# Two-layer hybrid block with expert lookup: the context tokens' routing moves beside the merge of the latent tokens, and GpSimd's adds and multiplies move to VectorE

## The chip, the cores and the metric

The kernel runs on one core of one Trainium2 chip. The metric is the time of one execution in microseconds (us). Before the change it is 4922.6 us (median of three runs, 4914.19 to 4927.8). The engines are TensorE (PE; its weight loads are PEld), VectorE (DVE), ScalarE (ACT), GpSimd (POOL) and SyncE (SP), which issues most of the transfers. The whole computation is in 32-bit floats.

## The reference, cut to what matters

There are 256 context tokens and 512 latent tokens, of width 1024, and two layers. In a layer each kind of token is normalized, projected, sent through three mixers (a state-space scan, differential attention, neighbourhood attention), and the three results are merged. After that comes an expert layer: every token scores 16,384 experts, takes the best 16 for each of 8 heads, and adds the weighted rows of those experts. In layer 1 only the latent tokens go on after the mixers.

```python
def merge_branches(y_ssm, y_diff, y_na, g_ssm, g_diff, g_na, w_br_ssm, w_br_diff, w_br_na, w_out):
    m = (sigmoid(g_ssm) * (y_ssm @ w_br_ssm) + sigmoid(g_diff) * (y_diff @ w_br_diff)
         + sigmoid(g_na) * (y_na @ w_br_na))
    return m @ w_out

def peer_ffn(h, wq, subkeys, u_tab, v_tab):              # h: normalized tokens
    q = (h @ wq).reshape(..., 8, 2, 128)
    s = einsum('bchxd,hxnd->bchxn', q, subkeys)           # scores of 128 + 128 half keys per head
    sv, si = top_k(s, 16)
    cand = sv[..., 0, :, None] + sv[..., 1, None, :]
    best, pos = top_k(cand, 16)
    eidx = take_along_axis(si0 * 128 + si1, pos)
    g = softmax(best)
    act = gelu(einsum('bchkd,bcd->bchk', u_tab[eidx], h))
    return einsum('bchk,bchkd->bcd', g * act, v_tab[eidx])

# in each layer, for latents (and for the context in layer 0):
x  = x + g1 * merge_branches(...)
h2 = rmsnorm(x, norm2_g) * (1 + sc2) + sh2
x  = x + g2 * peer_ffn(h2, ...)
```

## The kernel before, in words

**Arithmetic.** A 32-bit matmul operand is cut in two parts: ScalarE writes the rounded part `hi` (line 61) and VectorE the rest `lo = raw - hi` (line 62). `mm3` (lines 70 to 72) then runs three matmuls, hi by hi, lo by hi and hi by lo. Weights come in chunks of 128x1024 through a ring of `raw` tiles on SP's queue; `stream(3, 4)` gives three `raw` tiles and four pairs of parts. Each chunk therefore costs one transfer of 512 KB, one `hi` on ScalarE and one `lo` on VectorE before TensorE can use it.

**Stages of layer 0.** By the trace: a start (to 183 us), the mixers (to about 800), the merge (to 1093), a transition in which the tokens are normalized again (to 1138), the early stage (to about 2221), and the experts (to 2985). Layer 1 goes through the same stages with the latents alone.

**The merge** (`merge`, lines 924 to 972) works on one kind of tokens at a time, the 256 context tokens first (group 0), then the 512 latents (group 1). The mixer outputs are split into `yh` and `yl`. For each of eight blocks of 128 output columns, the three branches are multiplied by their weights (`w_br`), VectorE multiplies the result by the gate (line 946, tile `g`), and GpSimd adds the three (lines 947 and 948). The sum is split again into `mh` and `ml`, multiplied by `w_out`, scaled on VectorE (line 968, tile `d`) and added to the residual `x` on GpSimd (line 969). Beside the merge of layer 0, `modulation` multiplies 24 chunks of `ada_w` for layer 1; they use the same ring. The ring passes 80 chunks in this stage.

**The early stage** runs two things beside each other. `early` multiplies the latents by the 128 chunks of the expert table `peer_u` (tile `s`). `routing` first treats the context: normalization (`prepared`), queries with the 16 chunks of `peer_wq` (for 256 columns) and the scores of the half keys (`chosen`), the search for the best 16 by VectorE's maximum instructions (lines 1026 to 1033), the candidates and the lookup of their indices (`route`, lines 1064 to 1175), which leaves `picks`. Then it does the queries of the latents, and beside these `gathered` fetches for every pick of the context a row of the expert table per token: GpSimd issues an indirect transfer into one of five `grow` buffers (line 1200), and VectorE multiplies it with the token and sums (line 1214 for the first table, line 1222 for the second). What is left of the gathering goes on beside the experts.

**What sets the order.** `weave` draws pieces from several generators in proportion to the costs that they yield and to a budget for each. The order in which pieces are emitted and the framework's scheduler give every engine one list of instructions, which is fixed before the run. Instructions whose tiles share memory wait for one another; that includes transfers.

**Complex products** (`cmul`, lines 236 to 247, used in the start and the mixers) take six instructions; VectorE does four, and GpSimd a multiply (line 243) and, in most calls, an add (line 247).

Of the kernel before, what the change touches and what calls it, by code (L numbers as in the profile page):

```python
# [9 lines left out]
F32 = mybir.dt.float32  # L10
F32R = mybir.dt.float32r
# [10 lines left out]
LCTX, LLAT = 256, 512  # L22
# [28 lines left out]
class Net:  # L51
# [183 lines left out]

    def cmul(self, o, x, y, t, neg=False):

        v, g = self.nc.vector, self.nc.gpsimd
        v.tensor_mul(o[0], x[0], y[0])
        v.tensor_mul(t, x[1], y[1])  # L240
        v.tensor_sub(o[0], o[0], t)
        v.tensor_mul(t, x[0], y[1])
        g.tensor_mul(o[1], x[1], y[0])
        if neg:
            v.scalar_tensor_tensor(o[1], o[1], -1.0, t, op0=ALU.mult, op1=ALU.subtract)
        else:
            g.tensor_add(o[1], o[1], t)

    def exps(self, x, p, name, shape):

# [675 lines left out]
    def merge(self, l, x, t0, n, p):  # L926

        nc, v = self.nc, self.nc.vector
        ts = slice(t0, t0 + n)
        yh, yl, mh, ml = [p.tile([128, 8, n], F32R, name=a, bufs=1) for a in ("yh", "yl", "mh", "ml")]  # L930
        for k in range(8):
            t = p.tile([128, n], F32, name="yt")
            self.dma(t, self.ybuf[l][k, :, ts])
            self.split(t, yh[:, k], yl[:, k])
            yield 0.50
        for j in range(4):
            w = self.wchunk(self.a["w_br"][l, j])
            for h in range(2):
                c = slice(128 * h, 128 * h + 128)
                g = p.tile([128, 3, n], F32, name="g3")  # L940
                self.dma(g, self.gbuf[l][2 * j + h, :, :, ts])
                for b, (k0, nk) in enumerate(((0, 2), (2, 4), (6, 2))):
                    ps = self.ps1("mg")
                    self.mm3(ps[:, :n], lambda k: (w[0][:, k0 + k, c], w[1][:, k0 + k, c]),
                             lambda k: (yh[:, k0 + k], yl[:, k0 + k]), nk)
                    v.scalar_tensor_tensor(g[:, b], g[:, b], 1.0, ps[:, :n], op0=ALU.add, op1=ALU.mult)
                nc.gpsimd.tensor_add(g[:, 0], g[:, 0], g[:, 1])
                nc.gpsimd.tensor_add(g[:, 0], g[:, 0], g[:, 2])
                self.split(g[:, 0], mh[:, 2 * j + h], ml[:, 2 * j + h])
            yield 5.00  # L950
        tiles = range(t0 // 128, (t0 + n) // 128)
        gate = {}
        for r in sorted({1 if i < 2 else 0 for i in tiles}):
            gate[r] = p.tile([128, D], F32, name=f"g1{r}", bufs=1)
            self.dma(gate[r], self.arow[l][r:r + 1, 2 * D:3 * D].to_broadcast([128, D]))
        xt = {}
        for i in tiles:
            xt[i] = p.tile([128, D], F32, name=f"x{i - tiles[0]}", bufs=1)
            self.dma(xt[i], x[i])
        for j in range(4):  # L960
            w = self.wchunk(self.a["w_out"][l, j])
            c = slice(256 * j, 256 * j + 256)
            for i in reversed(tiles):
                t = slice(128 * i - t0, 128 * i - t0 + 128)
                ps = self.ps1("mg")
                self.mm3(ps[:, :256], lambda k: (mh[:, k, t], ml[:, k, t]), lambda k: (w[0][:, k], w[1][:, k]), 8)
                d = p.tile([128, 256], F32, name="d")
                v.scalar_tensor_tensor(d, ps[:, :256], 0.5, gate[1 if i < 2 else 0][:, c], op0=ALU.mult, op1=ALU.mult)
                nc.gpsimd.tensor_add(xt[i][:, c], xt[i][:, c], d)
            yield 4.00  # L970
        for i in reversed(tiles):
            self.dma(self.xs[i], xt[i])
# [353 lines left out]

    def front(self, l):

        x = self.a["x"] if l == 0 else self.xs
        kinds = range(l, 2)  # L1330
        with ExitStack() as right, ExitStack() as left:
            self.hidden(right.enter_context(self.pool("h", side="right")))
            own = right.enter_context(ExitStack())
            if l == 0:
                prep = self.ssm_prep(l, own.enter_context(self.pool("sprep", side="right")))
                with self.psum(mm=3, un=3, sm=2), self.pool("norm", 2) as p:
                    self.drain(self.weave((self.start(l, p), 40.0), (prep, 40.0), lead=True))
            else:
                prep = iter(())
                with self.pool("norm", 2, "right") as p:  # L1340
                    for i in range(6):
                        t = p.tile([128, 8, 128], F32, name="hn")
                        self.dma(t, self.hn[i])
                        self.part(128 * i, 128, t)

            def states():
                yield from prep
                own.close()
                with self.pool("ssm", 1, "right") as p:
                    yield from self.ssm(l, p)  # L1350
                if l < DEPTH - 1:
                    with self.pool("sprep", 1, "right") as p:
                        yield from self.ssm_prep(l + 1, p)

            def mixers(p):
                def attends(u):
                    for g in kinds:
                        yield from self.attend(l, g, u, p)

                cost = 84.0 if l == 0 else 72.0  # L1360
                yield from self.project(l, 0, p)
                yield from self.weave((self.project(l, 1, p), 48.0), (attends(0), cost))
                yield from self.weave((self.project(l, 2, p), 48.0), (attends(1), cost))
                yield from attends(2)

            pg = left.enter_context(self.pool("gate"))
            with self.stream(3, 4), self.psum(sc=2, mm=3, sm=2, gt=1), self.pool("att") as p:
                self.att_consts(l, p)
                self.drain(self.weave((mixers(p), 500.0 if l == 0 else 450.0), (states(), 300.0 if l == 0 else 200.0),
                                      (self.gates(l, pg), 187.0 if l == 0 else 125.0)))  # L1370
        with self.stream(3, 4), self.psum(mg=5, mm=3), self.pool("next", 2) as q:
            def merges():
                for g in kinds:
                    with self.pool("mg", 2) as p:
                        yield from self.merge(l, x, LCTX * g, LLAT if g else LCTX, p)

            jobs = [(merges(), 70.0)]
            if l < DEPTH - 1:
                jobs.append((self.modulation(l + 1, range(24), q), 72.0))
            self.drain(self.weave(*jobs))  # L1380

    def layer(self, l):
        self.front(l)
        own = (0, 1) if l == 0 else (2,)
        n = 512 if l == 0 else 384
        with self.pool("ga", 1, "right") as pa:
            rows = {i: pa.tile([128, D], F32, name=f"row{i}") for i in own}
            picks = {i: (pa.tile([128, 128], U32, name=f"pick{i}"), pa.tile([128, 128], F32, name=f"pw{i}")) for i in own}
            sums = self.gathered(l, own, rows, picks, pa)
            left = [256.0 * len(own)]  # L1390

            def counted():
# [5 lines left out]

            def routing():
                got = []  # L1400
                if l == 0:
                    with self.pool("route", 2) as p:
                        hc = [p.tile([128, 8, 256], F32R, name=a, bufs=1) for a in ("hch", "hcl")]
                        with self.pool("fin") as pn:
                            self.prepared(l, 0, hc, 0, rows, p, pn)
                        yield 5.0
                        yield from self.chosen(l, 0, 256, hc, got, p)
                        for i in own:
                            yield from self.route(l, *got[i], p, picks=picks[i])
                    got = []  # L1410
                with self.pool("route", 2) as p:
                    def rest():
                        if l == 0:
# [11 lines left out]
            with self.pool("h2", 1, "right") as ph, self.stream(ROWS, 4), self.psum(mm=4, s=4), self.pool("early", 2) as pe:  # L1425
                h2 = [ph.tile([128, 8, 512], F32R, name=a) for a in ("h2h", "h2l")]
                with self.pool("norm", 1) as p, self.pool("fin") as pn:
                    for i in (2, 4):
                        self.prepared(l, i, h2, 128 * (i - 2), rows, p, pn)
                self.drain(self.weave((routing(), 760.0 if l == 0 else 420.0), (self.early(l, h2, n, pe), 128.0)))  # L1430

            self.gate = {}
            late = [(i, rows[i]) for i in own]
# [121 lines left out]
```

## Time and profile before

| | us |
|---|---|
| median of 3 runs | 4922.6 |
| profiled execution, its own time | 4922.7 |
| span of the profiled execution | 4920.9 |
| TensorE busy | 4470.1 (91%) |
| VectorE busy | 3763.9 (76%) |
| ScalarE busy | 1845.4 (38%) |
| GpSimd busy | 1371.3 (28%) |

"Busy" counts instructions only, and a busy matmul includes some of its neighbour's time. Times that matter here are those at which a stage begins and ends, and the idle time of TensorE between and within the stages. In a row of the trace, `A<-B` is the output and its inputs by their names in the program; `x80` is a count; an arrow behind the idle time names what ended it.

### The profile page before, as it was taken

The page shows a single profiled execution, that of the slowest core. Times are in us where ns is not written, and L with a number is a line of the kernel's source. Part 1 is how long each engine was busy: PE and PEld are TensorE (multiplying, and loading weights), DVE is VectorE, ACT ScalarE, POOL GpSimd, SP SyncE. Part 2 cuts the span into 40 slices and gives each one's busy share as a digit, 9 for nine tenths or more (in the row PEclk, how much of TensorE's full clock was granted, in tenths as well). Part 3 has the DMA queues.
Part 4 walks back from the last instruction along what each step waited for, and adds up shares of the span by engine and source line. Part 5 has one row for each costly group of instructions (what it writes and reads, how often), then busy time and mean ns, then how long its engine had stood idle before and what let it go on. Part 6 is the DMA issues. An engine that isn't in the chain of part 4 may idle for free. (4 is left out here: it accounts for less than half of the span.)

```text
span 4920.9 us, 69116 instructions
## 1 busy us (share of the span) xinstructions
PE 4470.1 (91%) x24197; PEld 3733.3 (76%) x24197; DVE 3763.9 (76%) x8444; ACT 1845.4 (38%) x3019; POOL 1371.3 (28%) x1088
## 2 busy tenths in 40 slices
PE   7898898888998899887999997999769999989998
PEld 3687776677776787666888886877669999978887
DVE  8277885646888899997878854877545799978888
ACT  3144344424322254442222223445233355533333
POOL 4000210120265445643333310000200033334552
PEclk8999899898999999998999998999889999999999
DMA  5553434754598789999999965542434489999997
GB/s 203 168 149 101 133 123 131 238 187 148 200 329 315 265 315 341 340 333 373 367 341 345 347 213 173 149 131 94 162 124 138 156 324 350 342 331 386 367 378 269
DMA packets 462839, 1215.19 MB, mean 247 GB/s; under 512 B 47690, under 2 KB 181914, under 8 KB 458906
## 3 DMA queue, kind: packets, MB, share of 16 engines
q1 hardware_dynamic: 311002, 690.61, 41.3%
q0 software_dynamic: 110592, 402.70, 22.4%
q10 hardware_dynamic: 40896, 117.46, 6.1%
q8 instruction: 190, 3.11, 0.3%
q14 instruction: 159, 1.30, 0.1%
HBM read 1031.54 MB, written 179.04 MB: 246 GB/s over the span
## 5 line engine op out<-in xcount | busy, mean ns | idle before, releaser
L1200 POOL DMA_INDIRECT grow<-in_u_rows,pick x384 | 519.5, 1353 | 1223.8 <-DVE grow L1214 381.1
L61 ACT CAST hi<-raw 128x1024 fp32r<-128x1024 f32 x490 | 512.4, 1051 | 899.6 <-PE s L71 589.7
L62 DVE TENSOR_TENSOR lo<-raw,hi 128x1024 fp32r<-128x1024 f32 x490 | 606.6, 1241 | 314.2 <-ACT hi L61 307.6
L72 PE MATMUL s<-h2h,lo 128*128 128x512 f32 (+1 forms) x2048 | 764.7, 374 | 62.0 <-DVE lo L62 61.7
L1200 POOL DMA_INDIRECT grow<-in_v_rows,pick x384 | 608.2, 1584 | 695.5 <-PE stay L1271 236.2
L70 PE MATMUL s<-h2h,hi 128*128 128x512 f32 (+1 forms) x2048 | 773.0, 378 | 12.9 <-ACT eact L1238 8.3
L71 PE MATMUL s<-h2l,hi 128*128 128x512 f32 (+1 forms) x2048 | 761.2, 372 | 0.2 <-DVE h2l L62 0.2
L1268 PE MATMUL stay<-hiv,wh 128*128 128x512 f32 x1792 | 708.5, 396 | 46.9 <-ACT hiv L61 46.9
L1269 PE MATMUL stay<-lov,wh 128*128 128x512 f32 x1792 | 708.4, 395 | 0.0
L1271 PE MATMUL stay<-hiv,wl 128*128 128x512 f32 x1792 | 562.6, 395 | 0.0
L1222 DVE SCALAR_TENSOR_TENSOR row<-grow,gw,row 128x1024 f32<-128x1024 f32 x381 | 488.0, 1281 | 94.3 <-DMA grow<-in_v_rows,pick 91.6
L1214 DVE SCALAR_TENSOR_TENSOR grow<-grow,row 128x1024 f32<-128x1024 f32 x384 | 463.2, 1220 | 98.3 <-DMA grow<-in_u_rows,pick 97.7
L72 PEld LDWEIGHTS s<-h2h,lo 128*128 128x128 f32 x2048 | 391.7, 191 | 121.4 <-DVE lo L62 76.3
L61 ACT CAST wh<-w 128x512 fp32r<-128x512 f32 (+1 forms) x256 | 145.3, 568 | 784.4 <-DVE w L1258 379.6
L70 PEld LDWEIGHTS s<-h2h,hi 128*128 128x128 f32 x2048 | 392.7, 192 | 60.9 <-ACT eact L1238 13.4
L1268 PEld LDWEIGHTS stay<-hiv,wh 128*128 128x128 f32 x1792 | 338.4, 189 | 126.0 <-ACT hiv L61 47.4
L71 PEld LDWEIGHTS s<-h2l,hi 128*128 128x128 f32 x2048 | 391.7, 191 | 44.7 <-DVE h2l L62 0.6
L1269 PEld LDWEIGHTS stay<-lov,wh 128*128 128x128 f32 x1792 | 338.4, 189 | 80.2 <-DVE lov L62 1.3
L1271 PEld LDWEIGHTS stay<-hiv,wl 128*128 128x128 f32 x1792 | 338.1, 189 | 78.9
L62 DVE TENSOR_TENSOR lov<-raw,hiv 128x1024 fp32r<-128x1024 f32 x256 | 312.1, 1219 | 5.2 <-ACT hiv L61 4.9
L61 ACT CAST hiv<-raw 128x1024 fp32r<-128x1024 f32 x256 | 268.0, 1048 | 57.1 <-DMA raw<-in_peer_v 53.4
L1258 DVE TENSOR_TENSOR w<-act,gt 128x512 f32<-128x512 f32 (+1 forms) x256 | 158.8, 621 | 105.2 <-DMA act<-actd 103.7
(431 smaller groups left out, 8963.2 us busy)
## 6 DMA issues: line engine op xcount, KB each, us to landing
raw<-in_peer_u SPq DMA_DIRECT2D x256, 512.0 KB
raw<-in_peer_v SPq DMA_DIRECT2D x256, 512.0 KB
gd<-gst ACTq DMA_DIRECT2D x28, 2048.0 KB
raw<-in_w_in SPq DMA_DIRECT2D x88, 512.0 KB
actd<-eact ACTq DMA_DIRECT2D x128, 256.0 KB
gt<-gd SPq DMA_DIRECT2D x16, 2048.0 KB
act<-actd SPq DMA_DIRECT2D x128, 256.0 KB
adaw<-in_ada_w SPq DMA_DIRECT2D x48, 512.0 KB
```

The lines of the kernel that those rows point to most:

```text
L61: self.nc.scalar.copy(hi, x)
L62: self.nc.vector.tensor_sub(lo, x, hi.bitcast(F32))
L70: mm(ps, lh, rh, start=start and k == 0, stop=False)
L71: mm(ps, lh, rl, start=False, stop=False)
L72: mm(ps, ll, rh, start=False, stop=stop and k == n - 1)
L1200: d = nc.gpsimd.indirect_dma_start(out=t, out_offset=None, in_=self.a[table], in_offset=bass.IndirectOffsetOnAxis(ap=picks[y][0][:, j:j + ...
L1214: v.scalar_tensor_tensor(t, t, 1.0, h, op0=ALU.mult, op1=ALU.mult, accum_out=u[:, j:j + 1])
L1222: v.scalar_tensor_tensor(h, t, w[:, j:j + 1], h, op0=ALU.mult, op1=ALU.add)
L1258: v.tensor_mul(w.rearrange("p (b t) -> p b t", t=32), act.rearrange("p (b t) -> p b t", t=32), self.gt[:, :, i % 8])
L1268: nc.tensor.matmul(ps[:, c], wh[:, t], vh[:, c], start=i == 0, stop=False)
L1269: nc.tensor.matmul(ps[:, c], wh[:, t], vl[:, c], start=False, stop=False)
L1271: m = nc.tensor.matmul(ps[:, c], wl[:, t], vh[:, c], start=False, stop=i == 127)
```

## The change: what it does

Six things change, of which the third and fourth are about order.

1. In `cmul`, the multiply and the add of GpSimd become VectorE's.
2. In `merge`, the adds of `g` and of `x` become VectorE's. Each branch's product is added to the first as soon as it is there.
3. The residual tiles become one tile `xa` that takes the memory of `yh` (`tag="yh"`), and it is loaded behind the first chunk of `w_out`. Its transfer can thus begin only when the last branch matmul has read `yh`.
4. The merges leave `front` for a new function `merged`. Each kind of tokens has a `weave` of its own: group 0 with part of the modulation, group 1 with the rest of it and, in layer 0, with a generator `context` that holds the whole routing of the context tokens (normalization, queries, search, picks). This generator leaves the early stage.
5. The `grow` buffers of the gathering come from a pool that is opened behind the merge.
6. The budget of `routing` in the early stage of layer 0 is 665 in place of 760.

```diff
 def cmul(self, o, x, y, t, neg=False):
-        g.tensor_mul(o[1], x[1], y[0])
+        v.tensor_mul(o[1], x[1], y[0])
...
-            g.tensor_add(o[1], o[1], t)
+            v.tensor_add(o[1], o[1], t)
...
 def merge(self, l, x, t0, n, p):
                     v.scalar_tensor_tensor(g[:, b], g[:, b], 1.0, ps[:, :n], op0=ALU.add, op1=ALU.mult)
-                nc.gpsimd.tensor_add(g[:, 0], g[:, 0], g[:, 1])
-                nc.gpsimd.tensor_add(g[:, 0], g[:, 0], g[:, 2])
+                    if b:
+                        v.tensor_add(g[:, 0], g[:, 0], g[:, b])
...
-        xt = {}
-        for i in tiles:
-            xt[i] = p.tile([128, D], F32, name=f"x{i - tiles[0]}", bufs=1)
-            self.dma(xt[i], x[i])
         for j in range(4):
             w = self.wchunk(self.a["w_out"][l, j])
+            if j == 0:
+                xa = p.tile([128, len(tiles), D], F32, name="xa", tag="yh", bufs=1)
+                xt = {i: xa[:, i - tiles[0]] for i in tiles}
+                for i in tiles:
+                    self.dma(xt[i], x[i])
...
-                nc.gpsimd.tensor_add(xt[i][:, c], xt[i][:, c], d)
+                v.tensor_add(xt[i][:, c], xt[i][:, c], d)
...
+    def merged(self, l, context):
         with self.stream(3, 4), self.psum(mg=5, mm=3), self.pool("next", 2) as q:
-            def merges():
-                for g in kinds:
-                    with self.pool("mg", 2) as p:
-                        yield from self.merge(l, x, LCTX * g, LLAT if g else LCTX, p)
-
-            jobs = [(merges(), 70.0)]
-            if l < DEPTH - 1:
-                jobs.append((self.modulation(l + 1, range(24), q), 72.0))
-            self.drain(self.weave(*jobs))
+            mod = self.modulation(l + 1, range(24), q) if l < DEPTH - 1 else iter(())
+            for g in range(l, 2):
+                with self.pool("mg", 2) as p:
+                    jobs = [(self.merge(l, x, LCTX * g, LLAT if g else LCTX, p), 40.0)]
+                    if l < DEPTH - 1:
+                        jobs.append((mod, 48.0 if g else 22.0))
+                        if g:
+                            jobs.append((context, 98.0))
+                    self.drain(self.weave(*jobs, lead=g == 0))
...
 def layer(self, l):
-            sums = self.gathered(l, own, rows, picks, pa)
+            def context():
+                got = []
+                with self.pool("route", 2, "right") as p:
+                    hc = [p.tile([128, 8, 256], F32R, name=a, bufs=1) for a in ("hch", "hcl")]
+                    with self.pool("fin", 1, "right") as pn:
+                        self.prepared(l, 0, hc, 0, rows, pn, pn)
+                    yield 5.0
+                    yield from self.chosen(l, 0, 256, hc, got, p)
+                    for i in own:
+                        yield from self.route(l, *got[i], p, picks=picks[i])
+
+            self.merged(l, context())
+            sums = self.gathered(l, own, rows, picks, ex.enter_context(self.pool("gr", 1, "right")))
...
             def routing():
                 got = []
-                if l == 0:
-                    ...
-                        yield from self.chosen(l, 0, 256, hc, got, p)
-                        for i in own:
-                            yield from self.route(l, *got[i], p, picks=picks[i])
-                    got = []
...
-                self.drain(self.weave((routing(), 760.0 if l == 0 else 420.0), (self.early(l, h2, n, pe), 128.0)))
+                self.drain(self.weave((routing(), 665.0 if l == 0 else 420.0), (self.early(l, h2, n, pe), 128.0)))
```

The first place where the order of instructions differs is VectorE's list at the end of the latents' merge of layer 0. Before, it holds only `lo` parts of weights, the scalings `d` and copies for the modulation (`r_`):

```order
L62 TENSOR_TENSOR lo<-raw,hi 128x1024 x3
L968 SCALAR_TENSOR_TENSOR d<-mg,g_11129 128x256
L62 TENSOR_TENSOR lo<-raw,hi 128x1024
L968 SCALAR_TENSOR_TENSOR d<-mg,g_11129 128x256 x2
L62 TENSOR_TENSOR lo<-raw,hi 128x1024
L968 SCALAR_TENSOR_TENSOR d<-mg,g_11129 128x256
L62 TENSOR_TENSOR lo<-raw,hi 128x1024 x2
```

After the change (lines have moved by one) the same place of VectorE's list holds the adds to `xa` and, between them, the context's candidates (`cand`) and the search for the best of them (`best`, `pos`):

```order
L969 SCALAR_TENSOR_TENSOR d<-mg,g_11890 128x256
L1034 MAX_INDEX si_10404<-sv_10403,top_a 128x8
L970 TENSOR_TENSOR xa<-xa,d 128x256
L62 TENSOR_TENSOR lo<-raw,hi 128x1024
L1073 TENSOR_TENSOR cand<-sv_10403 128x8x16
L1073 TENSOR_TENSOR cand<-sv_10403 128x8x8
L969 SCALAR_TENSOR_TENSOR d<-mg,g_11890 128x256
L1073 TENSOR_TENSOR cand<-sv_10403 128x8x5
L970 TENSOR_TENSOR xa<-xa,d 128x256
```

What moved: the context's search stands among the weights' `lo` parts and the merge's own steps. The context's pieces come to 384 matmuls for the queries and 64 for the scores on TensorE, and to 16 more chunks in the ring, so that 96 pass it in the stage. Of the whole work of the context only the second tile's last lookups stand behind the last add to `xa`.

The second place is VectorE's list in the transition. Before, the normalization of a tile of latents is an unbroken chain, here from the sum of squares (`nss`) over the steps for the root (`nrst`, `nrs`) to the scaled tile `ny` and the second part `h2l`:

```order
L501 TENSOR_SCALAR nss<-nss 128x1
L509 TENSOR_SCALAR nrs<-nss 128x1
L512 TENSOR_TENSOR nrst<-nss,nrs 128x1
L513 SCALAR_TENSOR_TENSOR nrst<-nrst,nrs 128x1
L514 SCALAR_TENSOR_TENSOR nrs<-nrst,nrs 128x1
```

After the change the same chain has the gathering's multiply with sum (line 1215, formerly 1214) between its steps:

```order
L501 TENSOR_SCALAR nss<-nss 128x1
L1215 SCALAR_TENSOR_TENSOR grow,gu<-grow,row_9270 128x1024
L509 TENSOR_SCALAR nrs<-nss 128x1
L1215 SCALAR_TENSOR_TENSOR grow,gu<-grow,row_9270 128x1024
L512 TENSOR_TENSOR nrst<-nss,nrs 128x1
L513 SCALAR_TENSOR_TENSOR nrst<-nrst,nrs 128x1
L514 SCALAR_TENSOR_TENSOR nrs<-nrst,nrs 128x1
L1215 SCALAR_TENSOR_TENSOR grow,gu<-grow,row_9270 128x1024
```

Counted over the transition, 34 of these stand between the first sum of squares and the last `h2l`, and 8 more before the first `lo` of the early stage; before the change there is none up to the end of the context's routing. Between the start of the gathering and the first part of the experts' weights, VectorE's list holds 325 of them in both kernels.

## Rows read from the trace of the kernel before

**Rows 1.** The page: the span, and the group of line 1214.

```profile
span 4920.9 us, 69116 instructions
...
L1214 DVE SCALAR_TENSOR_TENSOR grow<-grow,row 128x1024 f32<-128x1024 f32 x384 | 463.2, 1220 | 98.3 <-DMA grow<-in_u_rows,pick 97.7
```

**Rows 2.** Stretches: length, busy PE PEld DVE ACT POOL, clock, DMA share, GB/s.

```profile
0.00:183.00 183.00, 143.99 (x704) 67.00 (x704) 118.43 (x456) 43.95 (x100) 60.95 (x102) 0.88 0.61 207
183.00:800.00 617.00, 567.86 (x3718) 495.46 (x3719) 457.04 (x1463) 259.60 (x636) 65.53 (x114) 0.96 0.38 118
822.00:1093.00 271.00, 233.77 (x1456) 188.98 (x1456) 154.17 (x185) 102.96 (x152) 67.76 (x55) 0.88 0.63 212
1093.00:1138.00 45.00, 9.41 (x41) 7.98 (x40) 25.74 (x91) 20.50 (x34) 0.72 (x1) 0.58 0.58 198
1138.00:2235.00 1097.00, 985.89 (x5092) 793.41 (x5092) 983.51 (x2374) 409.44 (x536) 499.12 (x326) 0.95 0.81 291
1284.00:1500.00 216.00, 200.38 (x861) 160.61 (x862) 190.49 (x550) 59.65 (x86) 115.87 (x82) 0.96 0.87 309
1900.00:2100.00 200.00, 176.06 (x957) 136.24 (x956) 195.70 (x379) 83.85 (x99) 121.06 (x71) 0.97 0.95 349
```

**Rows 3.** Tile `raw` in the merge: count, shortest/median/longest in ns, first and last start.

```profile
L61 ACT CAST hi<-raw x80: 1038/1046/1058, 822.9 to 1068.8; 128x1024 fp32r<-128x1024 f32 x80
```

**Rows 4.** VectorE's groups in the context's part, 1097 to 1290: count | busy, mean ns.

```profile
L62 DVE TENSOR_TENSOR lo<-raw,hi 128x1024 fp32r<-128x1024 f32 x31 | 37.9, 1224 | 36.9 <-ACT hi L61 36.9
L1033 DVE FIND_INDEX8 si<-sv,top_a 128x8 uint32<-128x128 f32 x32 | 9.2, 286 | 0.0
L1030 DVE FIND_INDEX8 pos<-best,cand 128x8 uint32<-128x50 f32 x15 | 3.1, 204 | 0.0
L1101 DVE TENSOR_TENSOR eq<-pf,starts 128x512 f32<-128x512 f32 x4 | 2.6, 682 | 0.0
```

**Rows 5.** GpSimd's groups, 183 to 1100: count | busy, mean ns.

```profile
L948 POOL TENSOR_TENSOR g<-g 128x512 f32<-128x512 f32 x8 | 14.6, 1821 | 2.8 <-DVE g L946 2.2
L243 POOL TENSOR_TENSOR big<-s,s 128x512 f32<-128x512 f32 x8 | 9.5, 1188 | 21.4 <-PE sm L442 10.7 <-PE sm L423 10.4
```

**Rows 6.** VectorE's group of the same shape in the mixers, 183 to 800.

```profile
L239 DVE TENSOR_TENSOR big<-s,s 128x512 f32<-128x512 f32 x8 | 5.5, 685 | 0.5 <-PE sm L423 0.5
```

**Rows 7.** Waits around the merge, 796 to 1105: total us, times, longest.

```profile
ACT mh L61 <- POOL g L948: 45.3, 15, 5.9
```

**Rows 8.** Waits of the early stage, 1138 to 2235.

```profile
PE s L72 <- DVE lo L62: 54.4, 29, 7.4
...
PE mm L72 <- DVE lo L62: 20.7, 7, 7.3
```

**Rows 9.** ScalarE and TensorE, single instructions: start, duration, [idle before].

```profile
1101.53 1.06 ACT L500 ACTIVATE ny<-nx 128x1024 f32<-128x1024 f32 x1 [31.65 <-DMA nx<-xs]
...
1138.23 1.22 PE L70 MATMUL s<-h2h,hi 128*128 128x512 f32 x2 [3.16 <-ACT h2h L61]
...
1151.16 0.28 PE L70 MATMUL mm<-hch,hi 128*128 128x256 f32 x1
1151.28 0.28 PE L71 MATMUL mm<-hcl,hi 128*128 128x256 f32 x1
...
2220.39 0.31 PE L1157 MATMUL mm<-oi,oj 128*128 128x128 f16 x1
```

**Rows 10.** GpSimd's first gathers, in order of time.

```profile
1290.23 0.94 POOL L1200 DMA_INDIRECT grow<-in_u_rows,pick  x1 [0.30 <-issue]
1317.31 1.68 POOL L1200 DMA_INDIRECT grow<-in_u_rows,pick  x1 [26.15 <-DVE grow L1214]
...
1336.62 0.94 POOL L1200 DMA_INDIRECT grow<-in_u_rows,pick  x1 [0.30 <-issue]
```

**Rows 11.** Transfers from 1290 to 2240, all queues together.

```profile
DMA packets 85728, 301.82 MB, mean 318 GB/s; under 512 B 9382, under 2 KB 11578, under 8 KB 83616
```

**Rows 12.** ScalarE in the merge of layer 1.

```profile
3552.56 1.05 ACT L61 CAST hi<-raw 128x1024 fp32r<-128x1024 f32 x1 [10.57 <-PE mg L72]
```

More of the change, by code (lines that the diff above doesn't have):

```diff
@@ L236, in cmul @@
     def cmul(self, o, x, y, t, neg=False):
-        v, g = self.nc.vector, self.nc.gpsimd
+        v = self.nc.vector
         v.tensor_mul(o[0], x[0], y[0])
@@ L1327, in front @@
     def front(self, l):
-        x = self.a["x"] if l == 0 else self.xs
         kinds = range(l, 2)
@@ L1370, in front @@
                                       (self.gates(l, pg), 187.0 if l == 0 else 125.0)))
+    def merged(self, l, context):
+        x = self.a["x"] if l == 0 else self.xs
         with self.stream(3, 4), self.psum(mg=5, mm=3), self.pool("next", 2) as q:
-            def merges():
-                for g in kinds:
-                    with self.pool("mg", 2) as p:
-                        yield from self.merge(l, x, LCTX * g, LLAT if g else LCTX, p)
-            jobs = [(merges(), 70.0)]
-            if l < DEPTH - 1:
-                jobs.append((self.modulation(l + 1, range(24), q), 72.0))
-            self.drain(self.weave(*jobs))
+            mod = self.modulation(l + 1, range(24), q) if l < DEPTH - 1 else iter(())
[7 more added lines that the diff above has]
+                    self.drain(self.weave(*jobs, lead=g == 0))
     def layer(self, l):
@@ L1385, in layer @@
         n = 512 if l == 0 else 384
-        with self.pool("ga", 1, "right") as pa:
+        with self.pool("ga", 1, "right") as pa, ExitStack() as ex:
             rows = {i: pa.tile([128, D], F32, name=f"row{i}") for i in own}
             picks = {i: (pa.tile([128, 128], U32, name=f"pick{i}"), pa.tile([128, 128], F32, name=f"pw{i}")) for i in own}
-            sums = self.gathered(l, own, rows, picks, pa)
+            def context():
[10 more added lines that the diff above has]
+            sums = self.gathered(l, own, rows, picks, ex.enter_context(self.pool("gr", 1, "right")))
             left = [256.0 * len(own)]
@@ L1400, in routing @@
                 got = []
-                if l == 0:
[L1402 to L1406, printed above, removed]
-                        yield from self.chosen(l, 0, 256, hc, got, p)
-                        for i in own:
-                            yield from self.route(l, *got[i], p, picks=picks[i])
-                    got = []
                 with self.pool("route", 2) as p:
```

## The prediction

> **What bounds the kernel now.** I read the stretches first, because the change touches only some stages: the start, the mixers, layer 0's merge, the transition behind it and the early stage [rows 2]. The reader is to see there which engine fills each stretch. In the mixers TensorE is busy 568 of 617 us. In the merge it is busy 234 of 271 us, VectorE 154; neither is full. In the transition, 45 us, TensorE is busy for 9. In the early stage VectorE is busy 984 of 1097 us and TensorE 986, so both are near their end, and what one waits for the other counts.
>
> The tile `raw` in the merge comes next: 80 chunks pass the ring from 822.9 to 1068.8 us, one per 3.07 us [rows 3]. Then the waits. In the merge ScalarE waits 45 us in 15 pieces for GpSimd's add [rows 7]. In the early stage TensorE waits 54.4 + 20.7 = 75 us for VectorE's `lo` [rows 8]. Last, single instructions at the two ends of the early stage: its first matmul is at 1138.2 and its last at 2220.4, 1082 us [rows 9].
>
> The sum below is made against the profiled execution's own time, 4922.7 us, which is 1.8 us over its span [rows 1] and 0.1 over the median of the three runs.
>
> **Merge of layer 0.** It gains 16 chunks in the ring; at 3.07 us each that is +49 if the ring's pace holds. VectorE's queue gives a second figure. It has 154 us now [rows 2]. The context's work adds 16 `lo` of 1.22, 32 key searches of five instructions of about 0.286, 16 searches of candidates of five of about 0.204, and for two tiles 48 lookups of about 0.68 [rows 4]: 20 + 46 + 16 + 33 = 115. Norm and small steps add to that, and I take 118. Of these, 15 lookups and some small steps, about 12 us, stand behind the merge's last add, so 106 count here. GpSimd's adds become VectorE's: 16 of 512 columns at 0.685 [rows 6], and 16 plus 24 of 256 columns, for which I take half, 11 + 14 = 25. So 154 + 106 + 25 = 285. How full can VectorE's queue be beside such a mixture of short steps and waits? At the share of 1900 to 2100 (0.98) 285 us take 291, which is +20; at the share of 1284 to 1500, 190/216 = 0.88, where key searches also run beside chunks, 324, +53; at that of the mixers, 457/617 = 0.74, 385, +114 [rows 2]. The nearest mixture is 0.88. Ring and queue nearly agree; I take **+50**. TensorE's part is no bound: 384 matmuls of 256 columns at 0.12 us [rows 9] and 64 for the scores, about as long, are 54 us, beside 234 in 271.
>
> GpSimd's adds are 1.82 us for 512 columns, VectorE's 0.685 [rows 5, 6], so the wait of 45 us before `mh` shrinks to a third. That is part of why the queue is not below 0.88.
>
> The load of `xa` is an added wait: SP holds it until the last branch matmul has read `yh`, and the later chunks stand behind it in SP's queue. After that 2 MB for the latents take 6.6 us at 318 GB/s [rows 11]. What covers it is the first chunk of `w_out`, which is there already: four tiles of 24 matmuls at 0.12 us [rows 9], 11.5 us of TensorE; for the context half of both. So I cost it at nothing; without the cover it would be 6.6 + 3.3 = +10. In layer 1 ScalarE has 10.6 us of slack at that place [rows 12]; there up to +5, against some -2 for the faster adds. I take 0.
>
> **Transition.** TensorE's gap is 45 us now. What moves into it is the gathering. In the new order of VectorE 42 multiply-and-sums of `grow` stand before the first `lo` of the early stage, where none stood. Five buffers can be fetched ahead; the other 37 come at the pace of the transfers. A gather is 512 KB, 1.65 us at 318 GB/s [rows 11]; GpSimd's first ten in a row come 1.93 us apart (1317.31 to 1336.62) [rows 10]. The normalization of four tiles lies beside it. Before it the tile must come back from memory: ScalarE's first step is 8.5 us into the gap [rows 9], about 10 us with the last add. So 10 + 37 x 1.65 = 71, **+26**; by the other pace 81, +36. Below: the context's own norm leaves the gap, and if the gathers start before the merge ends they cost only 42 x 1.22 = 51 of VectorE [rows 1], +10. Above: the second tile's lookups first (12), then 42 at 1.93: 103, +58.
>
> A row speaks against cheap interleaving: GpSimd waited 26.15 us for `grow` with four more landed behind it [rows 10], because the multiply that frees the buffer stood behind other work in VectorE's list. Nothing overtakes there. The Trainium skill, "TensorE: Matmul & The Clock Gate", section "Architectural detail: the array is 16× 32×32, not 1× 128×128", says the same of the vector and scalar engines, whose queues are strictly in order. By that rule a step of the root behind a gather that has not landed is late by the whole transfer; the row agrees, and it makes the third case below possible.
>
> **Early stage.** From its 1082 us the waits for `lo` go if VectorE is relieved, and the context's matmuls go. VectorE loses 118 us of context and the 42 multiplies (51 us): 984 - 169 = 815. TensorE's part: 1082 - 75 - 54 = 953. Some of the waits will come back, since 16 chunks fewer leave the ring but the gathering runs on; I take a quarter, 19, and get 972: **-110**. VectorE is then at 0.84, under both shares used above. Bounds: no waits come back, 953 (-129); all of them do, 1028 (-54).
>
> The budget of 665 gives the routing fewer pieces per chunk of `early`, as there is less of it; no cost of its own. The experts get the same remainder of the gathering (325 are done before them in both), so 0.
>
> **Start and mixers.** GpSimd's 61 us and 66 us [rows 2] are `cmul`, for the most part. On VectorE a multiply of 512 columns takes 0.685 in place of 1.19 [rows 5, 6], so some 70 us move to an engine that is busy 118 of 183 and 457 of 617. In the mixers TensorE covers it, with 568 of 617. In the start the chain of products gets shorter by each faster step while VectorE's queue gets longer. Bounds: -10, if these chains end the start, to +35, if half of it shows; I take **+8**, near the cover.
>
> **Sum.** 4922.7 + 50 + 26 - 110 + 8 + 0 = 4896.7; I say **4897**.
>
> **The rivals.**
> A. VectorE's queue in the merge fills badly: key searches stand between a chunk's `hi` and its `lo`, and with three raw tiles each delay stops the ring. Place: merge of layer 0. At the share 0.74 it takes 385 us, +114, and 4922.7 + 114 + 26 - 110 + 8 = 4961. For it: the merge is full of waits now, at a share of 0.57. Against: the context's short searches can fill just those waits. It is slower by over 0.3% from a merge of about +91 on (285 of 362 us, a share of 0.79).
> B. The gathers hold the normalization: lookups first, then 42 at 1.93 us, transition 103 us (+58). 4922.7 + 50 + 58 - 110 + 8 = 4929, no change to measure. For it: the order and the 26.15 us. Against: that pace was reached while key searches filled VectorE's list; in the transition it holds little but the norm.
> C. Everything fits: merge at 0.98 (+20) and no wait for `lo` left (-129). 4922.7 + 20 + 26 - 129 + 8 = 4848. For it: VectorE at 0.57 in the merge. Against: TensorE waits for transfers there too, the DMA share is 0.63.
> D. The change doesn't bring the context's work under the merge but behind it. The order speaks against it: all but 15 lookups stand before the last add. What would remain is the case of B.
>
> **How the numbers follow.** This kernel's measurement can tell about 0.3%, 15 us: faster is under 4908, slower over 4937. Chances: my case 0.48, A 0.18, B (with D) 0.20, C 0.14. My case alone reaches from 4865 to 4930, by a transition of +10 to +36, waits that come back from none to half, and -10 to +20 for the start; most of it is under 4908. From it 0.36 faster, 0.10 same, 0.02 slower; from A 0.15 slower, 0.03 same; from B 0.05 faster, 0.10 same, 0.05 slower; from C all faster, 0.14. Together 0.55, 0.23, 0.22. The range goes from C's time nearly to A's: 4848 to 4957.
>
> **What would show it.** In the new trace: the merge's end about 50 us later from its start, with VectorE's share near 0.88 and `raw` still one per 3 us; TensorE's gap behind it about 71 us, ended by the last `h2` and with gathers in VectorE's row; first to last matmul of the early stage about 972 us, with waits for `lo` under 40 us; the stage of the mixers within 10 us of its length. I am wrong if the merge grows by more than 90 us, if the gap passes 100, or if the early stage keeps its 75 us of waits: then VectorE wasn't what TensorE waited for.

## The result and the profile after

The changed kernel takes 4864.2 us (median of 4 runs, 4855.7 to 4878.6), the one before 4921.5 us in the same session (4 runs). The ratio is 0.9887, 95% interval 0.9859 to 0.9915: faster by 1.1%. The forecast was 4897, with 4848 to 4957. The profiled execution of the changed kernel is one of the slower ones: its span is 4876.8 us, 44.1 under the span of before [rows 1], while the medians differ by 57. Stages are compared by the profiles, whole kernels by the medians.

The page of the changed kernel, busy time of the engines:

```profile
span 4876.8 us, 68869 instructions
...
PE 4435.9 (91%) x24197; PEld 3722.9 (76%) x24197; DVE 3787.5 (78%) x8760; ACT 1844.3 (38%) x3015; POOL 1105.8 (23%) x772
```

VectorE does 316 instructions more than before and is busy only 24 us longer. The stretches of the changed kernel: length, busy time of PE, PEld, DVE, ACT and POOL, granted clock, DMA share, GB/s. They are start, mixers, merge, transition and early stage, and answer to the first five of [rows 2].

```profile
0.00:165.00 165.00, 134.61 (x704) 64.12 (x704) 119.09 (x554) 44.35 (x101) 0.20 (x4) 0.93 0.68 232
165.00:784.00 619.00, 577.32 (x3784) 505.02 (x3784) 457.55 (x1585) 264.20 (x647) 0.00 (x0) 0.97 0.40 123
...
790.00:1122.00 332.00, 278.41 (x1892) 240.38 (x1891) 264.10 (x735) 137.81 (x213) 1.17 (x1) 0.90 0.61 204
1122.00:1208.00 86.00, 12.34 (x64) 9.10 (x63) 72.74 (x168) 20.11 (x35) 48.58 (x37) 0.53 0.86 306
1208.00:2185.00 977.00, 913.21 (x4618) 735.42 (x4618) 841.06 (x1808) 367.51 (x464) 426.29 (x289) 0.96 0.81 296
```

In the start VectorE has 98 instructions more than before (554 against 456) and is busy for 119.1 us against 118.4. That is the line to stop at: work was added to it, and its time did not grow.

The table sets the stages of all kernels side by side, in us, from the starts of single matmuls: the first of the projections, the first and last of the merge, the first on `h2`, the first of the experts. "Early" includes the gap before the experts, "rest" is experts and layer 1. The last column is the median of the timed runs.

| kernel | start | mixers | merge | transition | early | rest | span | median |
|---|---|---|---|---|---|---|---|---|
| before | 184.6 | 648.6 | 259.5 | 45.5 | 1108.8 | 2673.9 | 4920.9 | 4921.5 |
| changed | 165.8 | 624.0 | 332.2 | 85.7 | 1000.5 | 2668.6 | 4876.8 | 4864.2 |
| cm_dve | 165.2 | 628.7 | 259.9 | 44.2 | 1108.1 | 2678.1 | 4884.2 | 4880.0 |
| mg_dve | 180.7 | 647.7 | 242.4 | 45.0 | 1103.0 | 2672.8 | 4891.6 | 4898.4 |
| noise | 185.9 | 652.7 | 262.1 | 45.6 | 1116.3 | 2678.0 | 4940.6 | 4931.7 |
| ctx_back | 166.6 | 620.4 | 238.3 | 46.4 | 1104.9 | 2666.7 | 4843.3 | 4846.0 |
| gather_late | 165.3 | 620.1 | 329.7 | 50.5 | 1023.8 | 2668.1 | 4857.5 | 4867.8 |
| search2 | 165.6 | 620.9 | 318.4 | 84.6 | 994.4 | 2670.2 | 4854.2 | 4852.4 |
| query2 | 164.5 | 622.0 | 317.9 | 87.3 | 993.1 | 2663.2 | 4848.0 | 4849.5 |
| ring4 | 164.3 | 621.6 | 311.2 | 82.8 | 988.9 | 2665.5 | 4834.3 | 4844.6 |
| late_norm | 167.1 | 622.3 | 332.4 | 86.8 | 991.0 | 2664.7 | 4864.3 | 4869.2 |
| ring4_late | 164.5 | 621.5 | 311.0 | 87.5 | 995.0 | 2665.7 | 4845.2 | 4847.2 |
| three | 166.4 | 621.2 | 312.1 | 53.6 | 1025.6 | 2664.8 | 4843.7 | 4844.7 |
| back_ring5 | 165.9 | 619.2 | 213.6 | 45.2 | 1116.6 | 2674.0 | 4834.5 | 4823.6 |

Before against changed: start and mixers -43, merge +73, transition +40, early stage -108, rest -5. The part of the change that moves the context's routing (merge, transition, early stage) comes to +5. The net gain of 44 us is thus, but for 1 us, that of the start and the mixers, in which only `cmul` changed.

### The profile page after: what moved, and what is told of

Read it like the earlier page. It is cut to its first block, busy times and chain, and to the rows that moved or that the text cites. A ratio compares the mean times of both kernels' runs of the same rounds, so it can differ in the third digit from the quotient of the medians.

```text
span 4876.8 us, 68869 instructions
## 1 busy us (share of the span) xinstructions
PE 4435.9 (91%) x24197; PEld 3722.9 (76%) x24197; DVE 3787.5 (78%) x8760; ACT 1844.3 (38%) x3015; POOL 1105.8 (23%) x772
## 5 line engine op out<-in xcount | busy, mean ns | idle before, releaser
L62 DVE TENSOR_TENSOR lo<-raw,hi 128x1024 fp32r<-128x1024 f32 x490 | 595.3, 1218 | 294.0 <-ACT hi L61 289.2
L1201 POOL DMA_INDIRECT grow<-in_v_rows,pick x384 | 581.2, 1514 | 730.4 <-PE stay L1272 262.3
```

Source lines behind the costliest of these rows:

```text
L62: self.nc.vector.tensor_sub(lo, x, hi.bitcast(F32))
L1201: d = nc.gpsimd.indirect_dma_start(out=t, out_offset=None, in_=self.a[table], in_offset=bass.IndirectOffsetOnAxis(ap=picks[y][0][:, j:j + ...
```

## The experiments

**Is the gain GpSimd's arithmetic or the move?** The first run changes `cmul` alone, in the kernel before.

```diff
-        g.tensor_mul(o[1], x[1], y[0])
+        v.tensor_mul(o[1], x[1], y[0])
...
-            g.tensor_add(o[1], o[1], t)
+            v.tensor_add(o[1], o[1], t)
```

> The kernel before with one edit: the multiply and the add of the complex products go from GpSimd to VectorE. Theory P (GpSimd's steps lay in the chains of the start and of the mixers, and slowed VectorE beside them): the start ends about 19 us earlier and the mixers give another 20 to 25, so -35 to -45 in all, about 4880 us. Theory R (the prediction's term: the work only moves, beside a full TensorE): -10 to +35 with +8 likeliest, about 4930 us.

It took 4880.0 us, ratio 0.9908 (0.9891 to 0.9924): -45. The start is 19 us shorter, the mixers 20. The prediction's term for this step, +8, is refuted.

The second run changes the merges' adds alone, in the kernel before.

```diff
-                nc.gpsimd.tensor_add(g[:, 0], g[:, 0], g[:, 1])
-                nc.gpsimd.tensor_add(g[:, 0], g[:, 0], g[:, 2])
+                    if b:
+                        v.tensor_add(g[:, 0], g[:, 0], g[:, b])
...
-                nc.gpsimd.tensor_add(xt[i][:, c], xt[i][:, c], d)
+                v.tensor_add(xt[i][:, c], xt[i][:, c], d)
```

> The kernel before with one edit: the adds of both merges go from GpSimd to VectorE; the x tiles stay as they are. Theory P: the wait of 45 us before mh shrinks to about 15 and the lo parts of the weights take 1.22 in place of 1.31 us; layer 1's merge gets about 12 us shorter and layer 0's 10 to 20, so about 4890 to 4900 us. Theory R (merge paced by its ring of chunks, layer 1's by TensorE): 0 to -2, about 4920 us.

It took 4898.4 us, ratio 0.9953 (0.9936 to 0.9969): -27, of which the merge of layer 0 shows 17 and that of layer 1 another 8.5 (from 116.3 to 107.8 us). VectorE's `lo` in the merge of layer 0, before and then in the run mg_dve (count | busy us, mean ns | idle time before):

```profile
L62 DVE TENSOR_TENSOR lo<-raw,hi 128x1024 fp32r<-128x1024 f32 x80 | 104.0, 1310 | 48.8 <-ACT hi L61 48.4
```

```profile
L62 DVE TENSOR_TENSOR lo<-raw,hi 128x1024 fp32r<-128x1024 f32 x80 | 97.4, 1222 | 43.8 <-ACT hi L61 43.6
```

The third run puts the context's routing back into the early stage and keeps the rest of the change.

```diff
-            self.merged(l, context())
+            self.merged(l)
...
             def routing():
+                if l == 0:
+                    ...
+                        self.prepared(l, 0, hc, 0, rows, p, pn)
+                        yield from self.chosen(l, 0, 256, hc, got, p)
+                        for i in own:
+                            yield from self.route(l, *got[i], p, picks=picks[i])
-                self.drain(self.weave((routing(), 665.0 if l == 0 else 420.0), (self.early(l, h2, n, pe), 128.0)))
+                self.drain(self.weave((routing(), 760.0 if l == 0 else 420.0), (self.early(l, h2, n, pe), 128.0)))
```

> The changed kernel with the context's routing put back into the early stage (budget 760 again); GpSimd has no arithmetic, the merges have their own weaves. Theory P: the move is worth about nothing (merge +73, transition +40, early stage -105 in the two traces), and all that was gained is GpSimd's arithmetic: 4845 to 4870 us, no slower than the changed kernel's 4864. Theory R (the prediction's terms: +50 +26 -110): the move is worth 34 us, so about 4898 us.

It took 4846.0 us, ratio 0.9853 (0.9833 to 0.9873). That is 18 us less than the changed kernel; as the two intervals overlap a little, what is shown is that the move gains nothing, not that it costs 18. The 34 us that the prediction's terms gave to it are excluded. The two single runs, -45 and -27, add up to -72; ctx_back has -79.

**Why does `cmul` on VectorE gain?** Either GpSimd's latency lay in the chains, or its arithmetic slows VectorE's. The run noise leaves `cmul` on VectorE and lets GpSimd do the same arithmetic into a scratch tile.

```diff
...
+        g.tensor_mul(scr, x[1][:, :cut], y[0][:, :cut])
         v.tensor_mul(o[1], x[1], y[0])
...
+            g.tensor_add(scr, scr, t[:, :cut])
             v.tensor_add(o[1], o[1], t)
```

> The run cm_dve (complex products all on VectorE), and beside each product GpSimd does the same multiply and add again into a scratch tile that nobody reads (of the largest ones three quarters). Nothing waits for its result. Theory chain (GpSimd's latency in the chains cost the 45 us): 4880 us as cm_dve, VectorE's steps as short as there. Theory contention (GpSimd's arithmetic slows VectorE's beside it, whoever reads the result): 20 to 45 us of the gain are lost, 4900 to 4925 us, and VectorE's 128x128 and 128x512 multiplies show longer means again.

It took 4931.7 us, ratio 1.0014 (1.0001 to 1.0027): the whole gain is gone. The same start with the same 554 instructions of VectorE, in cm_dve and then in noise (columns as above; one more instruction falls into the second window):

```profile
0.00:165.00 165.00, 132.97 (x704) 63.24 (x704) 119.02 (x554) 44.93 (x101) 0.20 (x4) 0.94 0.68 233
```

```profile
0.00:186.00 186.00, 144.59 (x705) 66.76 (x705) 134.31 (x555) 44.81 (x101) 55.85 (x102) 0.87 0.61 208
```

VectorE is busy 15 us longer for the same work, with GpSimd busy for 56 beside it. Over start and mixers together, up to the first matmul of the merge, it is 33 us, again cm_dve and then noise:

```profile
0.00:793.90 793.90, 716.86 (x4524) 571.80 (x4524) 581.74 (x2143) 314.11 (x755) 0.20 (x4) 0.95 0.46 148
```

```profile
0.00:838.60 838.60, 733.33 (x4525) 575.39 (x4525) 614.27 (x2140) 311.03 (x751) 122.09 (x216) 0.94 0.43 138
```

A single group can show it too: the four subtractions of `scb_s` (512 columns), in cm_dve and in noise. It is not typical: the products of the same tile (lines 249 and 254 of noise) keep their 679 ns.

```profile
L241 DVE TENSOR_TENSOR scb_s<-scb_s,s 128x512 f32<-128x512 f32 x4 | 2.7, 675 | 0.0
```

```profile
L251 DVE TENSOR_TENSOR scb_s<-scb_s,s 128x512 f32<-128x512 f32 x4 | 4.3, 1076 | 0.0
```

The experiment is not quite clean. GpSimd reads the tile `t`, and VectorE must wait before it writes it anew; such waits on `scr` come to about 15 us in VectorE's groups up to 840 us (8.7, 5.1 and 1.5). Start and mixers grow by 45 us against cm_dve. So contention is shown, by the longer durations; how the 45 us divide between it and these waits is not. In the kernel before, VectorE's waits for GpSimd in these stages come to 13 us, of the 39 us by which they are shorter in cm_dve; so these waits are not the whole gain.

**Does the gathering cost the transition?** GpSimd's first gather was held back until the last `h2l`.

```diff
-                        self.prepared(l, i, h2, 128 * (i - 2), rows, p, pn)
+                        last = self.prepared(l, i, h2, 128 * (i - 2), rows, p, pn)
+                if l == 0:
+                    self.pace = last        # the last h2l; a gather waits for self.pace
...
```

> The changed kernel with the gathers held back until the last h2l of the transition is written. Theory G (the gathers' multiplies stand in the norm's chain on VectorE and cost the 40 us by which the transition grew): TensorE's gap falls from 86 to 36 to 45 us; the 42 multiplies (51 us of VectorE) then lie in the early stage, which gives back 10 to 30: in all -10 to -30, 4835 to 4855 us. Rival 1 (the early stage is bound by VectorE and gives all back): gap shorter, time unchanged at 4864. Rival 2 (the gap is set by the last lookups and the reload of x, not by gathers): gap stays over 75 us, time unchanged.

It took 4867.8 us, ratio 0.9891 (0.9874 to 0.9907), as the changed kernel. TensorE's waits for the normalized tiles, in the changed kernel and then in gather_late (start, duration, idle time before and what ended it):

```profile
1142.55 1.97 PE L486 MATMUL mm<-ident,ny 128*128 128x128 f32 x8 [16.35 <-DVE ny L481]
1160.42 1.97 PE L486 MATMUL mm<-ident,ny 128*128 128x128 f32 x8 [15.90 <-DVE ny L481]
1183.91 1.94 PE L486 MATMUL mm<-ident,ny 128*128 128x128 f32 x8 [21.52 <-DVE ny L481]
1200.18 1.94 PE L486 MATMUL mm<-ident,ny 128*128 128x128 f32 x8 [14.33 <-DVE ny L481]
1207.68 1.22 PE L70 MATMUL mm<-h2h,hi 128*128 128x512 f32 x2 [5.56 <-ACT h2h L61]
```

```profile
1135.69 1.97 PE L486 MATMUL mm<-ident,ny 128*128 128x128 f32 x8 [16.30 <-DVE ny L481]
1144.54 1.97 PE L486 MATMUL mm<-ident,ny 128*128 128x128 f32 x8 [6.88 <-DVE ny L481]
1152.18 1.94 PE L486 MATMUL mm<-ident,ny 128*128 128x128 f32 x8 [5.67 <-DVE ny L481]
1159.76 1.94 PE L486 MATMUL mm<-ident,ny 128*128 128x128 f32 x8 [5.65 <-DVE ny L481]
1165.57 1.22 PE L70 MATMUL mm<-h2h,hi 128*128 128x512 f32 x2 [3.86 <-ACT h2h L61]
```

From tile to tile it is 16 to 23 us with the gathers between and 8 to 9 without: they cost the transition 35 us. But the early stage grows by 23, and the medians show nothing. What is gathered early is not gathered later.

**Why did the merge grow by 94 us** (238.3 in ctx_back, 332.2 in the changed kernel)? Three runs take something away, each from the changed kernel: search2 three of the five instructions of each key search, query2 six of eight blocks of the query matmuls, ring4 gives a fourth raw tile. The first two kernels thus leave out part of the result and serve only to time the merge.

```diff
+        if half:                            # search2, for the context
+            return
...
-                         lambda k: (h2[0][:, k, c0:c0 + n], h2[1][:, k, c0:c0 + n]), 8)
+                         lambda k: (h2[0][:, k, c0:c0 + n], h2[1][:, k, c0:c0 + n]), 2 if n == 256 else 8)        # query2
...
-        with self.stream(3, 4), self.psum(mg=5, mm=3), self.pool("next", 2) as q:
+        with self.stream(4, 4), self.psum(mg=5, mm=3), self.pool("next", 2) as q:        # ring4
```

> The changed kernel, but of the context's 32 key searches only the first two of five instructions are left (the best 8 of 16 keys; the others stand at a constant), so VectorE does 96 instructions of 0.28 us, 27 us, less in the merge. Theory queue (the merge grew by 94 us because VectorE's list is in order and the context's work delays lo and the merge's steps): merge 20 to 30 us shorter, 4835 to 4845 us. Theory ring (three raw tiles) and theory TensorE (54 us of added matmuls): under 8 us, about 4858 to 4864.

It took 4852.4 us (ratio 0.9838, 0.9822 to 0.9855); the merge is 14 us shorter, for 27 us of VectorE taken away.

> The changed kernel, but the context's queries sum over two of the eight blocks of 128 inputs: 288 matmuls of 256 columns, 35 us of TensorE, less in the merge; the chunks still pass the ring and are split. Theory TensorE (matmuls were added to an engine that is full between its waits): merge 25 to 35 us shorter, 4830 to 4840 us. Theories queue and ring: under 8 us.

It took 4849.5 us (0.9841, 0.9824 to 0.9857); the merge is 14 us shorter, for 35 us of TensorE. Its stretch can be set beside that of the changed kernel above (790 to 1122):

```profile
786.50:1104.40 317.90, 250.85 (x1605) 208.48 (x1605) 262.97 (x735) 137.43 (x213) 1.17 (x1) 0.89 0.63 213
```

TensorE is busy 28 us less and idle 13 us more (67 against 54).

> The changed kernel with four raw tiles in place of three in the merges (tile d has one buffer in place of two, to make room). Theory ring (96 chunks at the ring's pace): merge of layer 0 25 to 45 us shorter, 4820 to 4840 us. Theory queue or TensorE: 0 to 10 us shorter, 4855 to 4864 us.

It took 4844.6 us (0.9831, 0.9814 to 0.9848); the merge is 21 us shorter, under the 25 to 45 expected.

None of the three theories holds alone: of what is taken from VectorE or TensorE half or less comes back (14 of 27, 14 of 35), and the ring gives 21 of 94. These steps are clear of the scatter: in gather_late and late_norm, which leave the merge's work as it is, it takes 329.7 and 332.4 us, and in the three runs with a fourth raw tile 311.0 to 312.1. A fourth idea came from the trace. At the start of the latents' merge TensorE stood 13.1 and 6.7 us at the context's `ny`, with the granted clock at 0.71 from 862 to 915. The run late_norm puts the first branch matmuls ahead of it.

```diff
             def context():
                 got = []
+                yield 22.0
...
-                            jobs.append((context, 98.0))
+                            jobs.append((context, 120.0))
```

> The changed kernel, but the context's generator yields 22 before its normalization (budget 120 in place of 98), so that the first branch matmuls of the latents' merge stand ahead of the context's transposes on TensorE. Theory stall (at the start of the latents' merge TensorE's list stands at the context's ny for some 30 us, of the 94 by which the merge grew): that wait falls under 10 us, merge 15 to 25 us shorter, about 4840 to 4850 us. Rival (the ring would have stopped TensorE there anyway): merge within 8 us, about 4860.

It took 4869.2 us (0.9889, 0.9864 to 0.9913). TensorE's wait for `ny` in the merge fell from 19.8 to 6.4 us, and the merge stayed at 332: TensorE waits for `yh` and chunks there instead. My theory of this stall fell.

**Can the move be made to pay, or is there a better version?**

> ring4 and late_norm together. If they take away different waits: about 4844 - 15 to -25 = 4820 to 4830 us, below the 4846 of ctx_back, and moving the context's routing pays. If both take away the same wait: about 4844 us.

It took 4847.2 us (0.9839, 0.9818 to 0.9860): as ring4 alone.

> ring4_late with the gathers held back until the last h2l. By gather_late (4868, no change) the early stage gives back what the transition gains: the same as ring4_late within 8 us. If the early stage has room by now: 10 to 20 us below it.

It took 4844.7 us (0.9836, 0.9820 to 0.9851). With all three mends (a fourth raw tile, the later norm, the held gathers) the moved routing reaches what ctx_back has without any. The last run gives ctx_back five raw tiles, `self.stream(5, 4)` in `merged`.

> ctx_back (the context's routing in the early stage) with five raw tiles in the merges. Its merge waits 76 us on ScalarE for transfers of chunks (55 us ada_w, 10 each w_br and w_out). Theory ring: merge 15 to 30 us shorter, 4816 to 4831 us. Rival (TensorE is busy 214 of 238 us there): 0 to 10 us shorter, 4836 to 4846 us.

It took 4823.6 us (0.9790, 0.9772 to 0.9807), the fastest, below both kernels. Its merge is 25 us shorter. ScalarE's waits for chunks in that stage, in ctx_back and then in back_ring5 (total us, times, longest):

```profile
ACT hi L61 <- DMA raw<-in_ada_w: 55.2, 34, 4.3
...
ACT hi L61 <- DMA raw<-in_w_br: 10.3, 9, 2.3
ACT hi L61 <- DMA raw<-in_w_out: 10.2, 10, 2.6
```

```profile
ACT hi L61 <- DMA raw<-in_ada_w: 23.3, 18, 6.3
...
ACT hi L61 <- DMA raw<-in_w_br: 5.0, 4, 3.0
ACT hi L61 <- DMA raw<-in_w_out: 2.8, 3, 1.3
```

And the merges as a whole, ctx_back and back_ring5:

```profile
787.00:1025.00 238.00, 213.56 (x1410) 175.29 (x1410) 163.26 (x235) 100.99 (x146) 0.00 (x0) 0.93 0.71 239
```

```profile
785.00:999.00 214.00, 203.90 (x1417) 170.46 (x1415) 162.07 (x236) 98.22 (x146) 0.00 (x0) 0.98 0.77 264
```

With five raw tiles TensorE is busy 204 of 214 us and the granted clock is 0.98: TensorE has little left to wait for in that stage.

## Why the prediction was right, and where its steps were wrong

The sign and the range held, but by errors that cancel, which is luck. In the profile the sum was -26 and came out at -44.

**Early stage, -110: the size right, its two terms not.** First to last matmul took 977.4 us, 972 were forecast. The waits for `lo` came back to more than twice the quarter that I took (75 before, [rows 8]; 44 now), so they gave 31 us and not 56. TensorE's busy time fell by 73 us (985.9 in [rows 2], 913.2 after) where I took 54 for the context's matmuls. The two misses nearly cancel; 15 us of the other 19 lie in the 3072 matmuls of `early` (tile `s`, busy for 772 us before and 756 after); why these were shorter isn't shown. The waits after the change:

```profile
PE s L72 <- DVE lo L62: 31.6, 10, 4.9
...
PE mm L72 <- DVE lo L62: 12.1, 6, 3.6
```

**Transition, +26: the mechanism right, the size too small.** It is +40. I took the gathers to run from the end of the merge. GpSimd issued one at 1111 us and could not issue the second for 23 us:

```profile
1111.31 1.17 POOL L1201 DMA_INDIRECT grow<-in_u_rows,pick  x1 [1110.86 <-DVE key L1091]
1135.56 1.94 POOL L1201 DMA_INDIRECT grow<-in_u_rows,pick  x1 [23.08 <-DVE nss L501]
```

The first multiply is at 1142.4, 20 us into the gap and behind the last lookups; I had 10. From there 34 multiplies up to the first matmul on `h2` take 65 us, 1.9 us each, where I had 37 at 1.65. That wait for the last lookups is in rival B and not in my own case, and the gap (85.7) lies between the two (71 and 103).

**Merge, +50: mis-sized twice.** Against the kernel before it is +73. That hides -21 for the adds and the merges' own weaves (ctx_back against before; the adds alone give -17 in mg_dve), to which I gave no gain, and +94 for the context (the changed kernel against ctx_back). VectorE is busy for 264 us, where I had 285, and its share is 264/332 = 0.80, where I took 0.88 and where rival A began to decide (0.79). But A's mechanism, VectorE's queue alone, isn't what was found: 27 us less on VectorE gave 14. The ring's pace didn't hold either: its 96 chunks begin from 785.2 to 1111.9 us, one per 3.44 us, not 3.07. The step that failed is "TensorE's part is no bound". From ctx_back to the changed kernel TensorE is busy 65 us longer (213.6 to 278.4; I had 54) and idle 29 us longer, and in ctx_back it was already busy for 90% of that stage. That all of its added work came on top isn't shown, though: in query2 28 us less of it gave 14. The context's matmuls left the early stage and were paid, at least in part, in the merge. How the 94 us divide between TensorE, ring, VectorE's queue and clock stays open.

**Start and mixers, +8 (bounds -10 to +35): wrong, outside its bounds.** It was -43. I priced the moved work by VectorE's own 0.685 us and looked for its cover, and never asked what GpSimd's work did to VectorE's durations. The trace of before shows it in single instructions of the start, GpSimd's and VectorE's in order of time:

```profile
116.13 1.33 POOL L247 TENSOR_TENSOR big<-big,s 128x512 f32<-128x512 f32 x1
...
116.26 1.28 DVE L239 TENSOR_TENSOR rot<-rot,s 128x64 f32<-128x64 f32 x1
...
123.40 1.10 POOL L243 TENSOR_TENSOR big<-s,s 128x512 f32<-128x512 f32 x1
123.48 1.17 DVE L240 TENSOR_TENSOR rt<-rot,s 128x128 f32<-128x128 f32 x1 [0.63 <-POOL rot L247]
...
125.49 0.28 DVE L242 TENSOR_TENSOR rt<-rot,s 128x128 f32<-128x128 f32 x1
```

VectorE's product of 128x128 takes 0.28 us at 125.49, with nothing of GpSimd's beside it, and 1.17 us at 123.48, where it begins just behind one of GpSimd's. In both pairs VectorE's instruction ends within 0.15 us of GpSimd's end: it was held. Not every one is: up to 835 us, 40 of VectorE's two-input instructions of this shape ran beside one of GpSimd's, and 29 of them took what they take alone. The other 11 took 0.37 to 1.37 us; each began while GpSimd's was running and ended 0.15 us after it. The group of line 240 in the start, before and then in the changed kernel:

```profile
L240 DVE TENSOR_TENSOR rt<-rot,s 128x128 f32<-128x128 f32 x8 | 3.8, 470 | 2.4 <-POOL rot L247 2.4
```

```profile
L240 DVE TENSOR_TENSOR rt<-rot,s 128x128 f32<-128x128 f32 x8 | 2.2, 278 | 0.0
```

The Trainium skill, "GPSIMD Engine Reference", section "1. Specifications", says that GpSimd shares its ways into SBUF with VectorE, and that they contend where a VectorE instruction has two inputs there. The run noise agrees, with 134.3 against 119.0 us for the same work in the start.

**Layer 1 and the experts, 0.** They came out 5 us shorter. The merge of layer 1, to which I gave nothing, fell from 116.3 to 104.7 us; mg_dve shows 8.5 of it for the adds.

**The rivals.** Merge and transition together cost 37 us more than forecast (23 and 14), part of the way to A and to B; the 51 us by which `cmul` was mispriced covered them. **C** (4848) is nearer to the measured 4864 than my 4897, but none of its terms held: the merge is +73 and not +20, and 44 us of waits for `lo` are left. My own case was said to reach from 4865 to 4930; its bounds, added up, give 4844 to 4937. Of the signs that I named, four missed: VectorE's share in the merge, the ring's pace, the waits under 40 us (44), and the mixers within 10 us (25 shorter). **D**, that the change doesn't do what it says, was wrong as stated: the context's work does run beside the merge, it only isn't hidden there.

## What to carry to other kernels

Before work is moved under another stage, take that stage's bound as it is once the other edits are in: here TensorE was busy for 90% of the merge when GpSimd's adds were gone, and the context's work made it 94 us longer. For every GpSimd instruction with tensor operands, compare VectorE's durations of equal shape beside it and away from it, the longest ones too and not the median alone; what differs is a cost of GpSimd's that no busy share shows. A stage that gives back half or less of each of several reliefs has no single bound; here a deeper ring, a change of one or two lines, gave the most (21 and 25 us).

## What was not expected of the hardware

GpSimd arithmetic whose result nobody read cost as much as the arithmetic in use. In the start VectorE took over 98 instructions and was busy 0.7 us longer; with GpSimd working beside it into a tile that nobody reads, the same 554 instructions took 15 us more. Most of VectorE's instructions beside GpSimd's kept their time: up to the merge of noise some 445 ran beside one, and 81 of them took over 60 ns more than the median of their shape. The four subtractions of 128x512 went from 675 to 1076 ns in the mean.
